# A decoder layer on one core: activations laid out features first by the host, and the first norm's sum by squares and one product with ones

## The chip, the cores and the metric

The kernel runs on one core of one Trainium2 chip. The metric is device time in microseconds of one execution, the median of three runs. A core has five engines that work side by side, each with its own queue of instructions: TensorE (PE; its weight loads are listed as PEld), VectorE (DVE), ScalarE (ACT), GpSimd (POOL) and SyncE (SP), which here only issues transfers. ACT and POOL issue transfers too, on queues of their own.

## The reference, cut to what matters

One decoder layer runs on 256 prompt tokens and on 8 x 8 sample tokens that share the weights, 320 tokens in all, of 2048 features, in float32.

```python
xn = rms_norm(x, g_mix)
z = xn @ w_in            # 8704 columns: B, C, h, q, k, v, gate_c, gate_a
u = c_gate * h_conv
conv_out, conv_state = short_conv(u, conv_prev, w_conv)     # causal, width 3
y_conv = (b_gate * conv_out) @ w_conv_out
attn = ...               # window 128, 16 query and 4 kv heads, bias table, sinks
y_attn = attn @ w_attn_out
merged = sigmoid(gate_c) * y_conv + sigmoid(gate_a) * y_attn
h = x + merged @ w_o
hn = rms_norm(h, g_ffn)
h = h + (silu(hn @ w_gate) * (hn @ w_up)) @ w_down
y = rms_norm(h, g_final)
```

`rms_norm(x, g)` is `x * rsqrt(mean(x * x) + eps) * g`. For the sample group the keys are 128 cached ones of each sequence and 8 new ones, and the convolution starts from two cached rows. Besides y, the updated window of keys and values and the last two rows of u are returned.

## The kernel before

Everything is kept features first: a tile has 128 features as its partitions and the 320 tokens along its rows, and the 2048 features are 16 chunks. A product takes 128x128 of the weights as PE's stationary operand and streams the 320 tokens. Float32 is reached by splitting both sides in a rounded part and a rest (`xh` and `xl`, `whi` and `wlo`) and adding three products: `xh whi`, `xl whi`, `xh wlo`. So each weight tile is loaded by SP (`wraw`, four buffers), its `whi` is made by ACT (L94) and its `wlo` by DVE (L95; three buffers each).

The factor 1/rms is the same for all features of a token. So the products run on x times the gain, and the results are multiplied afterwards by `rb`, a tile that holds 1/rms of each token on all 128 partitions.

x comes in tokens first: three tiles `x0`, `x1`, `x2` of 128, 128 and 64 tokens, in five blocks of columns (`x_load`, L241). For each chunk PE transposes three pieces into PSUM (`x_turn`, L250, tile `pt`), ACT makes `xh` from it (L277; DVE for chunk 0, L275), DVE makes `xl` (L279) and copies x itself to `hT` (L286), which the residual needs later. The gain vector is transposed too (`pv`, L273, L274); `g_ffn` and the convolution's weights follow (`pw`).

The first stage is the product for keys and values (`kv_product`, L327): 16 chunks by 4 column blocks by 3 products, 192 in all, on weight tiles of 1, 1, 2, 2, ... chunks with 512 columns. In the course of a tile the x of the next tile is prepared (`x_prep`). Between products, `tick()` lets a generator of side work take one step. In this stage that is `start_rest`: eight small loads on POOL, which wait behind a copy of one column of `xh` of chunk 3 (`gate`, L344); the squares of x by rows on ACT (L362, twelve of them, each with a sum along the row); the bias table by a small product (`pe_`, L383), whose result `e_sb` goes to memory and back (`e_scr`, L387; `bias_s`, L398); the transposes of the convolution's state (`pst`, L394); and the norm. There 1/rms is worked out on 128x3 values (`rstd_of`, L184 to L196: scale and eps, root on ACT, reciprocal, and a step of refinement), put on the diagonals of three tiles `dg`, and spread over all partitions by three products with ones (`prb`, L409). After the stage `rb` is copied out of PSUM (L417), and the four accumulators are multiplied by it (`kT`, L419; `vT`, L421). Four PSUM banks hold accumulators (`acc`), so `q`, the next product, writes into banks that `kT` has to be read out of first.

Then come `q`, and `C`, `H`, `B` of the convolution, while the side work is attention. `sample_attention` loads the eight sequences' cached keys (`ck`, POOL), transposes them on PE (`pck`, L608, two to a sequence), copies them to `kf` together with the new keys (ACT, L609 and L610) and forms the scores (`pss`, L626). After that come the gates and output products (`gc`, `ga`, `yc`, `ya`), in whose first ticks `conv_state` transposes the last rows of u (`g18`, by `pg`, L837) and sends them out, then `wo`, and the feed-forward network in two halves (`fg`, `fu`, `dn`). The second norm takes its sum of squares by features: POOL squares and adds chunk after chunk (L909, L912, L913, tile `hacc`), one product with ones (`pss`, L992) adds over the partitions, and `rstd_of` runs on 128x320.

The program's order on each engine is laid down when it is built, by priority in the order of the source and by when a planner expects operands to be ready; `after(...)` puts an instruction behind given ones on their engines.

Of the kernel before, what the change touches and what calls it, by code (L numbers as in the profile page):

```python
# [8 lines left out]
F32 = mybir.dt.float32  # L9
# [6 lines left out]
D = 2048  # L16
TP, NB, TS = 256, 8, 8
T = TP + NB * TS
DC = 1024
# [17 lines left out]
LAG = 3  # L37
TOK = [(0, 128), (128, 128), (256, 64)]
# [3 lines left out]
def hybrid_layer(ctx: ExitStack, tc: tile.TileContext, a: dict, o: list):  # L42
    nc = tc.nc
    y_p, y_s, nk_p, nv_p, ncv_p, nk_s, nv_s, ncv_s = o
# [47 lines left out]

    def split_to(hi, lo, src):
        last["hi"] = nc.scalar.activation(hi, src, AF.Copy)  # L94
        last["lo"] = nc.vector.tensor_sub(lo, src, hi.bitcast(F32))  # L95
# [71 lines left out]
    vecs = cst.tile([P, 56], F32, name="vecs")  # L167
    g_mix = vecs[:, 0:16]
    g_ffn = vecs[:, 16:32]
    wcv = vecs[:, 32:56]  # L170
# [31 lines left out]
    hT = xp.tile([P, KC, T], F32, name="hT")  # L202
# [21 lines left out]
    vrow = st.tile([56, P], F32, name="vrow")  # L224
    g_in = nc.gpsimd.dma_start(vrow[0:16, :], a["g_mix"][0].rearrange("(k p) -> k p", p=P))
    with after(g_in):
        nc.gpsimd.memset(ident, 0.0)
    ident_in = nc.gpsimd.affine_select(
# [3 lines left out]
    xs = [st.tile([P, D], F32, name=f"x{t}") for t in range(3)]  # L232
    nc.vector.memset(xs[2][64:, :], 0.0)
    XB = [2, 2, 4, 4, 4]

    def x_load(i):
        cs = slice(sum(XB[:i]) * P, sum(XB[:i + 1]) * P)
        for t, (t0, tn) in enumerate(TOK):
            src = a["x_prompt"][0, t0:t0 + tn, :] if t < 2 else a["x_sample"].flatten_outer_dims()
            eng = nc.scalar if (i, t) in ((0, 1), (0, 2), (1, 2)) else nc.sync  # L240
            eng.dma_start(xs[t][:tn, cs], src[:, cs])  # L241

    x_load(0)
# [4 lines left out]
    def x_turn(kc, pt, tiles=range(3)):  # L248
        for t in tiles:
            last["x"] = nc.tensor.transpose(pt[:, t * P:(t + 1) * P], xs[t][:, kc * P:(kc + 1) * P], ident)  # L250

    def x_first():

        pts = [ps_aux(u("pt")) for _ in range(2)]
        for kc in range(2):
            x_turn(kc, pts[kc], (0, 1))
        with after(last["x"]):
            last["x"] = nc.tensor.matmul(wm, busy[:, :P], busy, start=True, stop=True)
        for kc in range(2):
            with after(last["x"]):  # L260
                x_turn(kc, pts[kc], (2,))
        last.pop("x")
        return pts

    def x_prep(kc, pt=None):
        if pt is None:
            pt = ps_aux(u("pt"))
            with after(last["mm"]):
                x_turn(kc, pt)
            last.pop("x")  # L270
        if kc == 0:
            pv = ps_aux("pv")
            nc.tensor.transpose(pv[:, 0:16], vrow[0:16, :], ident[:16, :16])  # L273
            mark["g"] = nc.vector.tensor_copy(g_mix, pv[:, 0:16])  # L274
            m1 = nc.vector.tensor_scalar(xh_t[:, kc, :], pt[:, :T], g_mix[:, kc:kc + 1], None, op0=ALU.mult)  # L275
        else:
            m1 = nc.scalar.activation(xh_t[:, kc, :], pt[:, :T], AF.Copy, scale=g_mix[:, kc:kc + 1])  # L277
        with after(*(mark[0][1:] if kc == 1 else ())):
            m2 = nc.vector.scalar_tensor_tensor(  # L279
                xl_t[:, kc, :], pt[:, :T], g_mix[:, kc:kc + 1], xh_t[:, kc, :].bitcast(F32),  # L280
                op0=ALU.mult, op1=ALU.subtract,
            )
        mark[kc] = (m1, m2)
        with after(*((last["lo"],) if kc < 2 and "lo" in last else ())):
            for k, p in [(kc, pt)] if kc > 1 else [(0, mark["pt"]), (1, pt)] if kc else ():
                nc.vector.tensor_copy(hT[:, k, :], p[:, :T])  # L286
        mark["pt"] = pt
# [3 lines left out]
    def load_kv(k0, n):  # L291
        raw = wp.tile([P, KT // 2, CK], F32, tag="wraw", name=u("wraw"), bufs=4)
        nc.sync.dma_start(
            raw[:, :n, :], w_in[k0 * P:(k0 + n) * P, O_K:O_K + CK].rearrange("(k p) n -> p k n", p=P)
        )
        hi = wp.tile([P, KT // 2, CK], F32R, tag="whi", name=u("whi"), bufs=3)
        lo = wp.tile([P, KT // 2, CK], F32R, tag="wlo", name=u("wlo"), bufs=3)
        with after(mark[1][0] if k0 == 2 else mark[k0][0], mark[k0][1]):
            split_to(hi[:, :n, :], lo[:, :n, :], raw[:, :n, :])
        return hi, lo  # L300

    def kv_product(tiles, x_after):
# [3 lines left out]
        pts = x_first()  # L306
        x_prep(0, pts[0])
        for i, n in enumerate(tiles):
            hi, lo = load_kv(k0, n)
            if i == 0:  # L310
                x_prep(1, pts[1])
# [5 lines left out]
            for k, c, m in passes(order, k0 + n == KC):  # L317
                kc = k0 + k
                if k0 + n == KC and (k, c, m) == (0, 2, 0):
                    tick()  # L320
# [5 lines left out]
                with after(*((mark["prb"],) if k0 + n == KC and c == 3 else ())):  # L326
                    last["mm"] = nc.tensor.matmul(  # L327
                        ps[c][:, :T], w[:, k, c * P:(c + 1) * P], x(kc),
                        start=(kc == 0 and m == 0), stop=(kc == KC - 1 and m == 2),
                    )  # L330
# [5 lines left out]
    srow = st.tile([2 * NB, DC], F32, name="srow")  # L336
# [5 lines left out]
    def small_loads():  # L342

        behind = nc.gpsimd.tensor_copy(gate, xh_t[:, 3, 0:1].bitcast(F32))  # L344
        with after(behind):
# [4 lines left out]
            nc.gpsimd.dma_start(vrow[16:32, :], a["g_ffn"][0].rearrange("(k p) -> k p", p=P))  # L350
            nc.gpsimd.dma_start(vrow[32:56, :], a["w_conv"][0].rearrange("j (c p) -> (j c) p", p=P))
            nc.gpsimd.dma_start(srow, a["state_conv"][0].rearrange("b j d -> (b j) d"))
            nc.gpsimd.dma_start(blk, a["c_block"])

    ss = st.tile([P, 3, 4], F32, name="ss")
    nc.vector.memset(ss, 0.5)

    def squares(*parts):
        for h, t in parts:
            tn = TOK[t][1]  # L360
            junk = wk.tile([P, 512], F32, tag="junk", name=u("junk"), bufs=1)
            nc.scalar.activation(  # L362
                junk[:tn, :], xs[t][:tn, h * 512:(h + 1) * 512], AF.Square, accum_out=ss[:tn, t, h:h + 1]
            )

    def start_rest():
        yield
        small_loads()
        yield
        with after(mark[3][0]):  # L370
            squares((0, 0), (0, 1))
        yield
        squares((0, 2), (1, 0))
        yield
        squares((1, 1), (1, 2))
        pw = ps_aux("pw")
        nc.tensor.transpose(pw[:, 0:56], vrow, ident[:56, :56])
        nc.vector.tensor_copy(vecs[:, 16:56], pw[:, 16:56])
        yield
        squares((2, 0), (2, 1), (2, 2))  # L380
# [8 lines left out]
        squares((3, 0), (3, 1), (3, 2))  # L389
        s3 = st.tile([P, 3], F32, name="s3")  # L390
        nc.vector.tensor_reduce(s3, ss, axis=AX.X, op=ALU.add)
        pst = ps_aux("pst")
        for c in range(8):
            nc.tensor.transpose(  # L394
                pst[:, c * 16:(c + 1) * 16], srow[:, c * P:(c + 1) * P], ident[:16, :16]
            )
        nc.vector.tensor_copy(st_sb.rearrange("p c s -> p (c s)"), pst[:, 0:128])
# [4 lines left out]
        r3 = rstd_of(s3, [P, 3], "r3", st)  # L402
        yield
        prb = ps_aux("prb")
        mark["rb"] = prb
        for t, (t0, tn) in enumerate(TOK):
            dg = st.tile([P, P], F32, name=f"dg{t}")
            nc.vector.tensor_scalar(dg[:tn, :tn], ident[:tn, :tn], r3[:tn, t:t + 1], None, op0=ALU.mult)
            mark["prb"] = nc.tensor.matmul(  # L409
                prb[:, t0:t0 + tn], ones[:tn, :], dg[:tn, :tn], start=True, stop=True  # L410
            )

    side_work[0] = start_rest()
    ps_kv = kv_product([1, 1] + [2] * 7, {0: (1,), 2: (2,), 3: (3,), 4: (4,)})
    for _ in side_work[0]:
        pass
    nc.vector.tensor_copy(rb, mark["rb"][:, :T])  # L417
# [6 lines left out]
    sp.close()  # L424

# [172 lines left out]
    def sample_attention(sm):  # L598
        def keys(b):
            ck = sm.tile([P, DKV], F32, tag="ckv", name=u("ck"), bufs=8)  # L600
            nc.gpsimd.dma_start(ck, a["cache_k"][0, b].rearrange("t h d -> t (h d)"))
            return ck

        def keys_t(b, ck):
            kf = sm.tile([P, 2, W2], F32, tag="kf", name=u("kf"), bufs=4)
            pk = ps_aux(u("pck"))
            for j in range(2):
                nc.tensor.transpose(pk[:, j * P:(j + 1) * P], ck[:, j * P:(j + 1) * P], ident)  # L608
            nc.scalar.activation(kf[:, :, 0:WIN], pk[:, 0:256].rearrange("p (j k) -> p j k", j=2), AF.Copy)  # L609
# [597 lines left out]
```

## Time and profile before

| | |
|---|---|
| median of 3 runs | 1690.38 us (1690.11 to 1690.67) |
| profiled execution | 1689.65 us, its span 1687.9 us |
| busy in the span | PE 1678.4, DVE 899.3, ACT 655.9, POOL 82.6 us |
| first `kv` product, first `q` product | 7.32 us, 43.13 us |
| moved | 258.16 MB, mean 153 GB/s |

How lines of the profile read: a timeline row is start, duration, engine, line, operation, result and operands, shapes and how many were merged; in brackets stand the idle time of the engine before it and what ended it. A row of groups gives the count, the busy time, the mean in ns, and the engine's idle time ahead of them. In a row of a window stand its length, then busy time and instructions of PE, PEld, DVE, ACT and POOL, the granted clock, the share of the transfer engines, and GB/s. Chain rows give start, length, and what the time went to. An `ACTq` or `SPq` is that engine's queue issuing a transfer.

### The profile page before, as it was taken

The page shows a single profiled execution, that of the slowest core. Times are in us where ns is not written, and L with a number is a line of the kernel's source. Part 1 is how long each engine was busy: PE and PEld are TensorE (multiplying, and loading weights), DVE is VectorE, ACT ScalarE, POOL GpSimd, SP SyncE. Part 2 cuts the span into 40 slices and gives each one's busy share as a digit, 9 for nine tenths or more (in the row PEclk, how much of TensorE's full clock was granted, in tenths as well). Part 3 has the DMA queues.
Part 4 walks back from the last instruction along what each step waited for, and adds up shares of the span by engine and source line. Part 5 has one row for each costly group of instructions (what it writes and reads, how often), then busy time and mean ns, then how long its engine had stood idle before and what let it go on. Part 6 is the DMA issues. An engine that isn't in the chain of part 4 may idle for free.

```text
span 1687.9 us, 26956 instructions
## 1 busy us (share of the span) xinstructions
PE 1678.4 (99%) x11103; PEld 1631.4 (97%) x11103; DVE 899.3 (53%) x1387; ACT 655.9 (39%) x944; POOL 82.6 (5%) x128
## 2 busy tenths in 40 slices
PE   9999999999999999999999999999999999999998
PEld 8999999999999999999999999998888999999887
DVE  7679564444444445556555555554444455555556
ACT  6455443333333333334333333333333333334344
POOL 2001211000000001330000000000000000000000
PEclk9999999999999999999999999999999999999999
DMA  7654545655545554444444444444444444444543
GB/s 228 174 153 135 171 143 157 179 150 150 150 150 150 150 150 150 150 150 150 150 150 150 150 150 150 150 149 151 150 150 150 150 150 150 150 150 150 175 142 109
DMA packets 238371, 258.16 MB, mean 153 GB/s; under 512 B 9210, under 2 KB 212822, under 8 KB 238120
## 3 DMA queue, kind: packets, MB, share of 16 engines
q1 hardware_dynamic: 235784, 250.25, 48.5%
q0 software_dynamic: 2160, 5.93, 1.3%
q8 instruction: 87, 1.43, 0.3%
q14 instruction: 36, 0.29, 0.1%
q10 hardware_dynamic: 304, 0.26, 0.1%
HBM read 253.29 MB, written 5.08 MB: 153 GB/s over the span
## 4 chain that ended last, share of the span: by engine, by line
PE 99%; DVE 0%; ACT 0%; issue 0%; DVEq 0%
PE fu L144 18%; PE fg L144 18%; PE dn L953 9%; PE wo L144 7%; PE gc L144 7%; PE ga L144 7%; PE dn L961 6%; PE C L144 3%; PE B L144 3%; PE H L144 3%; PE q L144 3%; PE yc L144 3%; PE ya L144 3%; PE dl L957 2%; PE kv L327 2%; PE dr L1110 1%
## 5 line engine op out<-in xcount | busy, mean ns | idle before, releaser
L95 DVE TENSOR_TENSOR wlo<-wraw,whi 128x1024 fp32r<-128x1024 f32 (+1 forms) x480 | 569.2, 1188 | 641.0 <-ACT whi L94 632.4
L94 ACT ACTIVATE whi<-wraw 128x1024 fp32r<-128x1024 f32 (+1 forms) x480 | 491.8, 1030 | 808.9 <-PE dn L953 179.0
L953 PE MATMUL dn<-a_t,whi 128*128 128x512 f32 x672 | 230.1, 395 | 0.0
L144 PE MATMUL fu<-hh_t,whi 128*128 128x320 f32 x704 | 212.4, 309 | 0.0
L144 PE MATMUL fg<-hh_t,whi 128*128 128x320 f32 x704 | 212.1, 308 | 0.0
L144 PE MATMUL fg<-hl_t,whi 128*128 128x320 f32 x704 | 212.1, 308 | 0.0
L144 PE MATMUL fu<-hl_t,whi 128*128 128x320 f32 x704 | 212.1, 308 | 0.0
L144 PE MATMUL fg<-hh_t,wlo 128*128 128x320 f32 x704 | 163.7, 308 | 0.0
L144 PE MATMUL fu<-hh_t,wlo 128*128 128x320 f32 x704 | 163.7, 308 | 0.0
L961 PE MATMUL dn<-a_t,wlo 128*128 128x320 f32 x672 | 158.7, 308 | 0.0
L953 PEld LDWEIGHTS dn<-a_t,whi 128*128 128x128 f32 x672 | 125.1, 188 | 24.4 <-issue 0.5
L144 PEld LDWEIGHTS fu<-hh_t,whi 128*128 128x128 f32 x704 | 132.1, 188 | 0.1
L144 PEld LDWEIGHTS fu<-hl_t,whi 128*128 128x128 f32 x704 | 132.0, 188 | 0.1
L144 PEld LDWEIGHTS fg<-hh_t,whi 128*128 128x128 f32 x704 | 132.1, 188 | 0.0
L144 PEld LDWEIGHTS fg<-hl_t,whi 128*128 128x128 f32 x704 | 132.1, 188 | 0.0
L961 PEld LDWEIGHTS dn<-a_t,wlo 128*128 128x128 f32 x672 | 117.9, 188 | 11.6
L144 PEld LDWEIGHTS fg<-hh_t,wlo 128*128 128x128 f32 x704 | 118.6, 188 | 0.0
L144 PEld LDWEIGHTS fu<-hh_t,wlo 128*128 128x128 f32 x704 | 118.6, 188 | 0.0
L144 PE MATMUL gc<-xh_t,whi 128*128 128x320 f32 x256 | 77.4, 310 | 0.0
L144 PE MATMUL ga<-xh_t,whi 128*128 128x320 f32 x256 | 77.4, 310 | 0.0
L144 PE MATMUL ga<-xl_t,whi 128*128 128x320 f32 x256 | 77.4, 310 | 0.0
L144 PE MATMUL gc<-xl_t,whi 128*128 128x320 f32 x256 | 77.3, 310 | 0.0
(305 smaller groups left out, 2773.0 us busy)
## 6 DMA issues: line engine op xcount, KB each, us to landing
wraw<-in_w_in_dram SPq DMA_DIRECT2D x119, 512.0 KB, 3.7
wraw<-in_w_gate_dram SPq DMA_DIRECT2D x88, 512.0 KB, 3.6
wraw<-in_w_up_dram SPq DMA_DIRECT2D x88, 512.0 KB, 3.6
wraw<-in_w_down_dram SPq DMA_DIRECT2D x88, 512.0 KB, 3.7
wraw<-in_w_o_dram SPq DMA_DIRECT2D x32, 512.0 KB, 3.6
wraw<-in_w_in_dram SPq DMA_DIRECT2D x34, 256.0 KB, 3.5
wraw<-in_w_conv_out_dram SPq DMA_DIRECT2D x16, 512.0 KB, 3.5
wraw<-in_w_attn_out_dram SPq DMA_DIRECT2D x32, 256.0 KB, 4.1
```

Of the source, the lines that this page charges most:

```text
L94: last["hi"] = nc.scalar.activation(hi, src, AF.Copy)
L95: last["lo"] = nc.vector.tensor_sub(lo, src, hi.bitcast(F32))
L144: last["mm"] = nc.tensor.matmul(ps[c][:, :T], w[:, k, c * P:(c + 1) * P], x(kc), start=(kc == 0 and i == 0), stop=(kc == nk - 1 and i == 2),)
L327: last["mm"] = nc.tensor.matmul(ps[c][:, :T], w[:, k, c * P:(c + 1) * P], x(kc), start=(kc == 0 and m == 0), stop=(kc == KC - 1 and m == 2),)
L953: nc.tensor.matmul(ps[c], parts[k][0][:, cs], a_t[:, k, 0:512], start=k == 0, stop=False)
L957: nc.tensor.matmul(low[:, :w], a_t[:, k, 512:], parts[k][0], start=k == 0, stop=k == nf - 1)
L961: last["mm"] = nc.tensor.matmul(ps[c][:, :T], parts[k][1][:, cs], a_t[:, k, 0:T], start=False, stop=k == nf - 1)
L1110: last["mm"] = nc.tensor.matmul(ps[:, :CW], x, w, start=(t == 2 and k == 0 and m == 0), stop=(k == nf - 1 and m == len(ms) - 1),)
```

## The change

The host lays out x (both groups), the two gain vectors with the convolution's weights, the convolution's state, and a copy of the cached keys features first, and puts the new convolution state back in order afterwards. On the chip:

- x comes straight into `hT`, now a part of a tile `xv` that begins with 56 columns of vectors, in eight blocks of 1, 1, 2, 2, 2, 2, 2 and 4 chunks, each one transfer of 128 partitions on SP. All transposes of x and of the vectors go, and with them the copies to `hT`. `xh` and `xl` read `hT`.
- The first two weight tiles are loaded on ACT's queue. In the first tile all products of one kind come before those of the next.
- ACT starts with a root of one column.
- The sum of squares: chunk by chunk ACT (even) or DVE (odd) squares 128x320, POOL adds it to `xacc`, and one product with ones adds over the partitions; `rstd_of` then runs on 128x320 and writes `rb` itself. It stands in the tile of chunks 12 and 13.
- The first splits of `q` are put behind the root on ACT and the last step of the norm on DVE (`first`).
- The state's transposes go; its load is direct. Two more small loads go.
- The cached keys are loaded by four transfers straight into `kf`, the new keys are added by two ACT copies, and the key transposes go. The scores keep their ticks.
- `g18` is sent out as it is; its transposes and copies go.

```diff
+VW = 56
+XB = [1, 1, 2, 2, 2, 2, 2, 4]
...
+    first = []
     def split_to(hi, lo, src):
-        last["hi"] = nc.scalar.activation(hi, src, AF.Copy)
-        last["lo"] = nc.vector.tensor_sub(lo, src, hi.bitcast(F32))
+        with after(*first):
+            last["hi"] = nc.scalar.activation(hi, src, AF.Copy)
+            last["lo"] = nc.vector.tensor_sub(lo, src, hi.bitcast(F32))
...
-    hT = xp.tile([P, KC, T], F32, name="hT")
+    xv = xp.tile([P, VW + KC * T], F32, name="xv")
+    g_mix, g_ffn, wcv = xv[:, 0:16], xv[:, 16:32], xv[:, 32:VW]
+    hT = xv[:, VW:].rearrange("p (k t) -> p k t", k=KC)
...
+    def x_load(i):
+        c0, c1 = (VW + sum(XB[:j]) * T if j else 0 for j in (i, i + 1))
+        nc.sync.dma_start(xv[:, c0:c1], a["x_v"][:, c0:c1])
+    x_load(0)
+    x_load(1)
+    first_root = st.tile([P, 1], F32, name="first_root")
+    nc.scalar.activation(first_root, ones[:, 0:1], AF.Sqrt)
...
+    def x_prep(kc):
         if kc == 0:
-            pv = ps_aux("pv")
-            nc.tensor.transpose(pv[:, 0:16], vrow[0:16, :], ident[:16, :16])
-            mark["g"] = nc.vector.tensor_copy(g_mix, pv[:, 0:16])
-            m1 = nc.vector.tensor_scalar(xh_t[:, kc, :], pt[:, :T], ...)
+            m1 = nc.vector.tensor_scalar(xh_t[:, kc, :], hT[:, kc, :], ...)
         else:
-            m1 = nc.scalar.activation(xh_t[:, kc, :], pt[:, :T], AF.Copy, ...)
+            m1 = nc.scalar.activation(xh_t[:, kc, :], hT[:, kc, :], AF.Copy, ...)
...
     def load_kv(k0, n):
-        nc.sync.dma_start(
+        (nc.scalar if k0 < 2 else nc.sync).dma_start(
...
+            seq = passes(order, k0 + n == KC)
+            if i == 0:
+                seq.sort(key=lambda kcm: kcm[2])
+            for k, c, m in seq:
...
-                if k0 and (k, c, m) == (0, 3 if n > 1 else 1, 0) and k0 + n < KC:
+                if k0 and (k, c, m) == (0, 1 if n == 1 or k0 + 2 * n == KC else 3, 0) and k0 + n < KC:
                     x_prep(k0 + n)
                     x_prep(k0 + n + 1)
                     tick()
...
-            nc.scalar.activation(
-                junk[:tn, :], xs[t][:tn, h * 512:(h + 1) * 512], AF.Square, accum_out=...
-            )
+    xacc = st.tile([P, T], F32, name="xacc")
+    def squares(*chunks):
+        for k in chunks:
+            t = xacc if k == 0 else st.tile([P, T], F32, tag="sq", name=u("sq"), bufs=4)
+            if k % 2 == 0:
+                nc.scalar.activation(t, hT[:, k, :], AF.Square)
+            else:
+                nc.vector.tensor_mul(t, hT[:, k, :], hT[:, k, :])
+            if k:
+                nc.gpsimd.tensor_tensor(xacc, xacc, t, op=ALU.add)
...
     def start_rest():
+        squares(0)
         yield
         small_loads()
+        squares(1)
+        yield
+        squares(2, 3, 4)
+        yield
+        squares(5, 6, 7)
+        yield
+        squares(8, 9, 10, 11)
         ...              # nsink, pe_, e_sb, e_scr as before
         yield
+        squares(12, 13, 14, 15)
+        yield
         ...              # bias_s as before
         yield
         prb = ps_aux("prb")
+        nc.tensor.matmul(prb[:, :T], ones, xacc, start=True, stop=True)
+        rstd_of(prb[:, :T], [P, T], "r1", st, out=rb)
...
-    nc.vector.tensor_copy(rb, mark["rb"][:, :T])
...
+    first += [last["root"], last["inv"]]
...
+        kf = sm.tile([P, NB, 2, W2], F32, name="kf")
+        for h in range(0, NB, 2):
+            nc.gpsimd.dma_start(kf[:, h:h + 2, :, 0:WIN], a["cache_kt"][:, h:h + 2])
...
-            ps = product(load_q(j, gp), KC, xh, xl, "q")
+            ps = product(load_q(j, gp), KC, xh, xl, "q", loaded=first.clear)
...
-                nc.tensor.transpose(pg[:18, i * P:(i + 1) * P], g18[:, h * 4 + i, :], ident)
-            nc.vector.tensor_copy(n18[:, h * 512:(h + 1) * 512], pg[:18, :])
...
+        nc.gpsimd.dma_start(ncv, g18)
```

More of the change, by code (lines that the diff above doesn't have):

```diff
@@ L231, in hybrid_layer @@
     )
[L232 to L243, printed above, removed]
     wm = ps_aux("wm")
@@ L247, in hybrid_layer @@
         nc.tensor.matmul(wm, busy[:, :P], busy, start=True, stop=True)
[L248 to L270, printed above, removed]
+    def x_prep(kc):
         if kc == 0:
-            pv = ps_aux("pv")
-            nc.tensor.transpose(pv[:, 0:16], vrow[0:16, :], ident[:16, :16])
-            mark["g"] = nc.vector.tensor_copy(g_mix, pv[:, 0:16])
-            m1 = nc.vector.tensor_scalar(xh_t[:, kc, :], pt[:, :T], g_mix[:, kc:kc + 1], None, op0=ALU.mult)
-        else:
[L277 to L281, printed above, removed]
-            )
+            m1 = nc.vector.tensor_scalar(xh_t[:, kc, :], hT[:, kc, :], g_mix[:, kc:kc + 1], None, op0=ALU.mult)
+        else:
+            m1 = nc.scalar.activation(xh_t[:, kc, :], hT[:, kc, :], AF.Copy, scale=g_mix[:, kc:kc + 1])
+        m2 = nc.vector.scalar_tensor_tensor(
+            xl_t[:, kc, :], hT[:, kc, :], g_mix[:, kc:kc + 1], xh_t[:, kc, :].bitcast(F32),
+            op0=ALU.mult, op1=ALU.subtract,
+        )
         mark[kc] = (m1, m2)
[L284 to L287, printed above, removed]
     CK = 2 * DKV
@@ L325, in kv_product @@
                 w, x = ((hi, xh), (hi, xl), (lo, xh))[m]
[L326 to L330, printed above, removed]
+                last["mm"] = nc.tensor.matmul(
+                    ps[c][:, :T], w[:, k, c * P:(c + 1) * P], x(kc),
+                    start=(kc == 0 and m == 0), stop=(kc == KC - 1 and m == 2),
+                )
             k0 += n
@@ L388, in start_rest @@
         yield
[L389 to L397, printed above, removed]
+        squares(12, 13, 14, 15)
+        yield
         nc.gpsimd.dma_start(
@@ L401, in start_rest @@
         yield
-        r3 = rstd_of(s3, [P, 3], "r3", st)
-        yield
         prb = ps_aux("prb")
[L405 to L411, printed above, removed]
+        nc.tensor.matmul(prb[:, :T], ones, xacc, start=True, stop=True)
+        rstd_of(prb[:, :T], [P, T], "r1", st, out=rb)
     side_work[0] = start_rest()
-    ps_kv = kv_product([1, 1] + [2] * 7, {0: (1,), 2: (2,), 3: (3,), 4: (4,)})
+    ps_kv = kv_product([1, 1] + [2] * 7, {0: (2,), 2: (3,), 3: (4,), 4: (5, 6), 5: (7,)})
     for _ in side_work[0]:
         pass
-    nc.vector.tensor_copy(rb, mark["rb"][:, :T])
     for c in range(2):
@@ L598, in sample_attention @@
     def sample_attention(sm):
[L599 to L609, printed above, removed]
-            nc.scalar.activation(kf[:, :, WIN:W2], kT[:, :, TP + b * TS:TP + (b + 1) * TS], AF.Copy)
-            return kf
+        kf = sm.tile([P, NB, 2, W2], F32, name="kf")
@@ new lines, in sample_attention @@
+        new = kT[:, :, TP:T].rearrange("p j (b t) -> p b j t", b=NB)
+        for j in range(2):
+            nc.scalar.activation(kf[:, :, j, WIN:W2], new[:, :, j], AF.Copy)
+        yield
+        yield
+        for base in range(0, NB, 3):
+            ps = ps_aux(u("pss"))
+            n = min(3, NB - base)
+            for b in range(base, base + n):
+                o0 = (b - base) * W2
+                for kv in range(NKV):
+                    j, par = kv // 2, kv % 2
+                    rows = slice(par * 64, par * 64 + 64)
+                    nc.tensor.matmul(
+                        ps[kv * 32:(kv + 1) * 32, o0:o0 + W2], qs[rows, j, b, :], kf[rows, b, j, :],
+                        start=True, stop=True,
+                    )
+            nc.vector.tensor_add(
+                s[:, base:base + n, :], ps[:, 0:n * W2].rearrange("p (b k) -> p b k", b=n),
+                flip(bias_s).unsqueeze(1).to_broadcast([P, n, W2]),
+            )
@@ L1205 @@
     r = _run(nc, [arrays], core_ids=[0])
-    return tuple(r.results[0][f"out_{i}_dram"] for i in range(len(_OUTS)))
+    res = [r.results[0][f"out_{i}_dram"] for i in range(len(_OUTS))]
+    ncv = _np.asarray(res.pop()).transpose(2, 1, 0)
+    res.insert(4, ncv[:2].reshape(1, 1, 2, DC))
+    return (*res, ncv[2:].reshape(1, NB, 2, DC))
```

89 lines of the change are left out of this document (18 added, 71 removed).

## The prediction

> **What bounds the kernel now.** I read the page first: the span, and the chain that ended last.
>
> ```profile
> span 1687.9 us, 26956 instructions
> ...
> PE 99%; DVE 0%; ACT 0%; issue 0%; DVEq 0%
> ```
>
> TensorE (PE) is the chain from end to end, so whatever leaves its stream leaves the time, unless something else becomes late in its place. The profiled execution took 1689.65 us, 1.75 more than its span; the median of the three runs is 1690.38, 0.73 above it. I work out differences on the trace and take them off 1690.38.
>
> The unit price is in the chain itself, where a whole stretch has no wait in it:
>
> ```profile
> 267.06 14.08 PE H L144 x96
> ```
>
> 96 products of 128x128 weights with 320 tokens in 14.08 us are 0.147 us each. The change is nearly all in the first stage, the product for keys and values (`kv`), so I read its chain from 0 to 46 us, its first and last product in the timeline, and its window:
>
> ```profile
> by line: PE kv L327 64.1%; PE pt L250 12.5%; PE wm L247 6.9%; PE q L144 6.1%; PE prb L409 1.8%; PE pst L394 1.3%; DVE xh_t L275 1.2%; DVE busy L163 1.1%; PE wm L258 0.9%; issue 0.9%; PE pe__406 L383 0.7%; PE pw L377 0.4%; DVE vecs L274 0.4%
> ```
>
> ```profile
> 0.74 0.40 ACTq L241 DMA_DIRECT2D x<-in_x_prompt_dram  x1
> ...
> 1.20 0.44 SPq L293 DMA_DIRECT2D wraw<-in_w_in_dram  x1
> ...
> 4.75 0.63 ACT L94 ACTIVATE whi<-wraw 128x512 fp32r<-128x512 f32 x1 [1.10 <-DMA wraw<-in_w_in_dram]
> ...
> 7.32 0.82 PE L327 MATMUL kv<-xh_t,whi 128*128 128x320 f32 x4 [0.94 <-DVE xh_t L275]
> ...
> 8.87 1.06 ACT L94 ACTIVATE whi<-wraw 128x1024 fp32r<-128x1024 f32 x1 [1.20 <-DMA wraw<-in_w_in_dram]
> ...
> 43.13 0.31 PE L144 MATMUL q<-xh_t,whi 128*128 128x320 f32 x1
> ```
>
> ```profile
> 0.00:7.50 7.50, 5.09 (x16) 2.60 (x17) 3.48 (x7) 2.79 (x4) 1.44 (x9) 1.00 0.76 229
> 0.00:8.85 8.85, 6.44 (x25) 3.96 (x26) 4.83 (x10) 2.96 (x4) 1.44 (x9) 1.00 0.80 251
> 7.32:43.13 35.81, 35.81 (x251) 34.56 (x252) 28.81 (x61) 25.60 (x53) 8.08 (x15) 1.00 0.78 227
> ```
>
> The stage has 192 kv products, 28.2 us at 0.147, but runs 35.81 us, from 7.32 to 43.13. The chain says what fills the rest: `pt`, the transposes of x, 12.5% of 46 us or 5.8; `prb` 0.8, `pst` 0.6, and `pe_` 0.3. VectorE (DVE, third pair of the window row) is busy for 28.81 of the 35.81 us. That is the number to keep in mind: PE is the bound, but DVE is the next one.
>
> **The start.** Three waits stand ahead of the first product at 7.32: the transposes, the gain vector's transpose with its copy, and xh by DVE. With x and gains already feature first, only a load and one DVE pass are left for x, and the first weights decide. Those were issued at 1.20 on SP and used at 4.75, after 3.55 us. They move to ACT's queue, whose first transfer went out at 0.74: there at 4.29, split (0.63) at 4.92, first product at about 5.1, 2.2 us earlier. That is not all kept. The third weight tile (two chunks) could be split at 8.87 before. Ahead of it must come four chunks of x and four of weights, 0.16 and 0.26 MB each, and 0.03 MB of vectors: 1.73 MB, the same as before in another order. The windows say 229 GB/s over the first 7.5 us, 1.72 MB. So it lands between 7.5 and 8.87; I take 8.0, as nothing now has to wait for later chunks of x. Its split (1.06) ends at 9.1. PE, having done 24 products from 5.1, would be there at 8.6; so the third tile starts at 9.1.
>
> **What PE has left.** From 9.1: 14 chunks of 12 products, 168 x 0.147 = 24.7, plus the table product `pe_` and the one product with ones, 0.3 and some 0.8 (the six records of `prb`, also plain f32, took 0.8): the stage could end at 34.9. Against 43.13 that is 8.2 us. Whether it does depends on DVE.
>
> **What DVE gets.** Its groups between 9.1 and 43.1 us:
>
> ```profile
> L95 DVE TENSOR_TENSOR wlo<-wraw,whi 128x1024 fp32r<-128x1024 f32 x7 | 8.5, 1212 | 0.0
> L279 DVE SCALAR_TENSOR_TENSOR xl_t<-pt,vecs,xh_t 128x320 fp32r<-128x320 f32 x14 | 7.6, 545 | 4.7 <-ACT xh_t L277 4.7
> ```
>
> The copies of 16 transposed chunks out of PSUM go. There stay seven `wlo` (8.5) and, after 9.1, twelve `xl` at 0.545 (6.5). New are seven of the eight odd squares and the chain that makes 1/rms, which was on 128x3 values and now runs on 128x320. The same chain on that shape is in the trace, for the second norm:
>
> ```profile
> L192 DVE RECIPROCAL r<-r 128x320 f32<-128x320 f32 x1 | 2.2, 2159 | 0.5 <-ACT r L191 0.5
> ...
> L194 DVE TENSOR_TENSOR r<-r,r 128x320 f32<-128x320 f32 x1 | 0.5, 494 | 0.0
> L196 DVE SCALAR_TENSOR_TENSOR rb<-r,r 128x320 f32<-128x320 f32 x1 | 0.5, 483 | 0.0
> L184 DVE TENSOR_SCALAR r<-pss 128x320 f32<-128x320 f32 x1 | 0.5, 482 | 0.0
> L193 DVE SCALAR_TENSOR_TENSOR r<-r 128x320 f32<-128x320 f32 x1 | 0.5, 479 | 0.0
> ```
>
> That is 2.16 + 0.49 + 0.48 + 0.48 + 0.48 = 4.1. Squares at the price of such a tensor product, 7 x 0.49 = 3.4. For the small steps that stay (the e_sb table, nsink) I allow 0.8. So 8.5 + 6.5 + 3.4 + 0.8 + 4.1 = 23.3 us of DVE's own work.
>
> **What Pool's adds cost DVE.** Fifteen adds of 128x320 on Pool are new here, fourteen after 9.1. The nearest rows are the second norm's sums, first on Pool, then what DVE did at the same time:
>
> ```profile
> 661.03 0.72 POOL L912 TENSOR_TENSOR sq<-hT 128x320 f32<-128x320 f32 x1 [9.45 <-DVE hT L902]
> 661.83 1.04 POOL L913 TENSOR_TENSOR hacc<-hacc,sq 128x320 f32<-128x320 f32 x1
> 662.83 1.75 POOL L912 TENSOR_TENSOR sq<-hT 128x320 f32<-128x320 f32 x1
> ```
>
> ```profile
> 661.58 0.55 DVE L904 SCALAR_TENSOR_TENSOR hl_t<-hT,vecs,hh_t 128x320 fp32r<-128x320 f32 x1 [0.63 <-ACT hh_t L903]
> ...
> 663.92 1.01 DVE L904 SCALAR_TENSOR_TENSOR hl_t<-hT,vecs,hh_t 128x320 fp32r<-128x320 f32 x1
> ```
>
> The two engines hold each other up. A Pool operation takes 0.72 when it meets little of DVE and 1.75 beside a `wlo`; the DVE operation takes 1.01 instead of 0.55 after meeting Pool, 0.46 more. The bounds for an add are therefore nothing (it falls in an idle gap of DVE) and 0.72 (DVE stands for all of it); I take the measured 0.46: 14 x 0.46 = 6.4.
>
> [...]
>
> **The sum.** DVE is through its list at 9.1 + 23.3 + 6.4 = 38.8, and the first key bank must then be scaled before `q` may write into it, 0.5: `q` starts at 39.3 instead of 43.13, 3.8 us earlier. PE's own 34.9 is covered by it. ACT loses its twelve row squares and gets eight of 128x320, and stays behind both. The wait put on the first splits of `q` (behind the root on ACT and the last step of the norm on DVE) costs nothing by itself as those two come before the scaling that `q` needs anyway; what is queued behind them is the first `q` tile. Pool's adds stand in one queue with six loads and the e_scr transfer:
>
> ```profile
> 10.99 0.19 POOL L344 COPY gate<-xh_t 128x1 f32<-128x1 f32 x1 [8.47 <-ACT xh_t L277]
> ...
> 14.74 0.56 POOL L353 DMA_DIRECT2D blk<-in_c_block_dram  x1
> 28.99 0.52 POOL L387 DMA_DIRECT2D e_scr<-e_sb  x1 [13.68 <-DVE e_sb L386]
> ```
>
> The gate can open some 2 us earlier, six loads at about 0.55 end near 12.3, and fourteen adds at 1.04, the middle row, with 0.5 for e_scr, end at 27.4: before the product with ones is due.
>
> Later parts, both on the chain between dense products, so that removing them is all gain (chains of 200 to 228 us, and from 296):
>
> ```profile
> by line: PE C L144 50.3%; PE H L144 27.4%; PE pss L626 8.1%; PE B L144 7.3%; PE pck L608 7.3%
> ```
>
> ```profile
> 298.74 0.87 PE pg L837 x8
> ```
>
> The key transposes are 7.3% of 28 us, 2.0; the conv state's are 0.9. What replaces them is four loads on Pool instead of eight and two ACT copies instead of sixteen; the scores stay at the same ticks.
>
> Together 3.8 + 2.0 + 0.9 = 6.7 us: 1683.7.
>
> **Rivals.** *PE stays the bound.* DVE idled for 7.0 us of the old stage (35.81 - 28.81); if the adds fall into such gaps and the chain on 128x320 runs beside the last tile, the stage ends at 34.9 and the gain is 8.2 + 2.9 = 11.1: 1679.3. Against it: DVE's list alone is 23.3 of 25.8 us. 0.27.
>
> [...] Each add costs DVE 0.72: 10.1 instead of 6.4, `q` at 43.0, the stage gains nothing and only the later parts remain: 1687.4. [...] 0.20 with what lies between.
>
> *Pool's queue stops PE (slower).* e_scr waited until 28.99 for e_sb. If eight adds queue behind it, from 29.5 at 1.75 (the row beside a `wlo`) they end at 43.5. The product with ones stands in PE's queue ahead of the last 45 kv products, so PE stands still: 43.5 + 0.6 + 6.6 = 50.7, 7.6 later than before, less 2.9: 1695.1. It decides for slower when the last add ends after 42.2. For it: one queue, one chain of sums. Against it: half the adds come ahead of e_scr, and e_sb can come earlier as its loads do. 0.05.
>
> **How the numbers follow.** The forecast has 0.45, with `q` between 37 and 41.5. The range runs from the first rival, 1679, to past the second, 1688; it leaves out the third and 0.03 for what I don't see. This kernel's runs differ by some 0.03%; 0.2%, or 3.4 us, is about what can be told from no change. Faster by more means below 1687.0: the forecast, the first rival and half of the second, 0.82. Within it the other half and the unseen, 0.13. Slower 0.05.
>
> **What would show it.** Right: first kv product near 5.1, third tile near 9.1, no `pt`, `pck`, `pg` on PE; DVE over 90% busy from there until `q`; `wlo` and `xl` lengthened beside Pool's adds; PE gaps of some 4 us in the stage, ended by `wlo` or `xl`; `q` near 39.3. Wrong: PE gaps ended by Pool's last add (third rival), or no gaps at all (first).

## The result and the profile after

The changed kernel takes 1690.89 us, the median of 14 runs (1689.51 to 1691.37), against 1690.43 (1689.14 to 1691.18) for the kernel before in 14 runs: a ratio of 1.0001, 95% interval 0.9994 to 1.0009. The forecast was 1683.7, with a range from 1679.0 to 1688.0. Nothing was gained that can be measured, and the measured time lies outside the range.

The profiled execution took 1691.36 us. Its page, the span and the chain that ended last:

```profile
span 1689.3 us, 26708 instructions
...
PE 98%; DVE 1%; DMA 0%; POOL 0%; issue 0%; SPq 0%; ACT 0%; DVEq 0%; POOLq 0%
```

The span is 1.4 us longer than before, and the chain, which was PE with hardly anything else, now has a percent of DVE and traces of Pool. They lie in the first stage. Its timeline on PE, with the first products, the first product after each of the two long gaps, and the window of the stage:

```profile
5.15 1.44 PE L296 MATMUL kv<-xh_t,whi 128*128 128x320 f32 x4 [0.52 <-ACT whi L99]
...
9.58 0.47 PE L296 MATMUL kv<-xh_t,whi 128*128 128x320 f32 x1
9.85 0.47 PE L296 MATMUL kv<-xl_t,whi 128*128 128x320 f32 x1
...
11.24 0.31 PE L296 MATMUL kv<-xh_t,whi 128*128 128x320 f32 x1
11.38 0.31 PE L296 MATMUL kv<-xl_t,whi 128*128 128x320 f32 x1
...
23.34 0.31 PE L296 MATMUL kv<-xl_t,whi 128*128 128x320 f32 x1
25.24 0.42 PE L296 MATMUL kv<-xh_t,wlo 128*128 128x320 f32 x1 [1.59 <-DVE wlo L100]
...
28.74 0.31 PE L296 MATMUL kv<-xl_t,whi 128*128 128x320 f32 x1
33.81 0.64 PE L296 MATMUL kv<-xh_t,wlo 128*128 128x320 f32 x1 [4.77 <-DVE wlo L100]
```

```profile
5.15:10.64 5.49, 5.49 (x20) 5.49 (x21) 4.66 (x8) 4.81 (x10) 2.96 (x6) 1.00 1.00 374
5.15:45.70 40.55, 34.19 (x196) 33.10 (x197) 36.20 (x46) 20.38 (x37) 24.19 (x28) 0.92 0.65 212
31.12:37.95 6.83, 4.14 (x15) 4.14 (x16) 6.50 (x6) 0.00 (x0) 3.32 (x4) 0.50 0.63 168
```

The first product came at 5.15 as forecast, 2.17 earlier than before. But `q` starts at 45.70, 2.57 later than before: the stage lasts 40.55 us instead of 35.81. Four things fill it beside its 28.2 us of products at full pitch. The first twenty products take 5.49 us, 0.27 each (9.58 to 9.85) where later ones take 0.147, 2.5 more than at that pitch; the clock's records begin at 10.64, at full speed, and ahead of the first one the column shows 1.00 for these products too, so there the pitch has to tell: it is that of the products from 34.24 to 37.18, in the stretch granted half. PE stands for 1.90 and for 5.07 us start to start, both times until a `wlo` comes from DVE; 6.7 less the two products themselves. From 31.12 to 37.95 the clock is granted at half, and the 18 products behind the second gap take 4.76 us (the chain, below), 2.1 too many. `prb` and `pe_` make 0.8. That is 28.2 + 2.5 + 6.7 + 2.1 + 0.8 = 40.3 of the 40.55.

What DVE did ahead of the second gap is in the chain of waits:

```profile
23.57 1.61 DVE wlo L100
25.18 2.16 DVE xl_t L253 x2
27.34 0.80 DVE sq L330
...
29.75 1.14 DVE xl_t L253
30.89 1.07 DVE sq L330
31.96 1.81 DVE wlo L100
...
33.81 4.76 PE kv L296 x18
38.58 0.54 PE prb L360 x2
```

The `wlo` that PE needs stands in DVE's queue behind four `xl` and two squares of later chunks, and each of these takes about twice what it takes without Pool beside it (`xl` 0.55 us, a square 0.48, in the run without adds below). The groups of the first 46 us on DVE and Pool:

```profile
L253 DVE SCALAR_TENSOR_TENSOR xl_t<-xv,xh_t 128x320 fp32r<-128x320 f32 x16 | 12.8, 832 | 0.0
L100 DVE TENSOR_TENSOR wlo<-wraw,whi 128x1024 fp32r<-128x1024 f32 x7 | 10.8, 1558 | 0.5 <-ACT whi L99 0.5
L330 DVE TENSOR_TENSOR sq<-xv 128x320 f32<-128x320 f32 x8 | 5.8, 738 | 1.3 <-POOL xacc L332 1.3
```

```profile
L332 POOL TENSOR_TENSOR xacc<-xacc,sq 128x320 f32<-128x320 f32 x15 | 16.8, 1120 | 1.3 <-DVE sq L330 0.5
```

`xl` takes 832 ns where it took 545 before, `wlo` 1558 for 1212, and an add on Pool 1120. ACT, which was to stay behind, waits as well; its waits from 9 to 30 us:

```profile
ACT sq L328 <- POOL xacc L332: 5.6, 3, 2.1
```

Three squares on ACT stand for 5.6 us until an add on Pool lets go of one of the four `sq` buffers, and in ACT's order the next `xh` and `whi` stand behind them.

### The profile page after: what moved, and what is told of

It is laid out like the page before. It is cut to its first block, busy times and chain, and to the rows that moved or that the text cites. A ratio compares the mean times of both kernels' runs of the same rounds, so it can differ in the third digit from the quotient of the medians.

```text
span 1689.3 us, 26708 instructions
## 1 busy us (share of the span) xinstructions
PE 1673.3 (99%) x11016; PEld 1626.4 (96%) x11016; DVE 903.9 (54%) x1367; ACT 647.4 (38%) x914; POOL 95.8 (6%) x135
## 4 chain that ended last, share of the span: by engine, by line
PE 98%; DVE 1%; DMA 0%; POOL 0%; issue 0%; SPq 0%; ACT 0%; DVEq 0%; POOLq 0%
PE fg L149 18%; PE fu L149 18%; PE dn L883 9%; PE ga L149 7%; PE wo L149 7%; PE gc L149 7%; PE dn L891 6%; PE H L149 3%; PE C L149 3%; PE B L149 3%; PE q L149 3%; PE ya L149 3%; PE yc L149 3%; PE dl L887 2%; PE dr L1040 1%; PE kv L296 1%
## 5 line engine op out<-in xcount | busy, mean ns | idle before, releaser
L149 PE MATMUL wo<-m_h,whi 128*128 128x320 f32 x256 | 77.2, 309 | 0.0
```

Source lines behind the costliest of these rows:

```text
L149: last["mm"] = nc.tensor.matmul(ps[c][:, :T], w[:, k, c * P:(c + 1) * P], x(kc), start=(kc == 0 and i == 0), stop=(kc == nk - 1 and i == 2),)
```

## The experiments

Two theories stand against each other. **A**: the loss comes from Pool's adds, through the time that they and DVE take from each other and through the `sq` buffers that they hold. **B**: it comes from the squares themselves, work added to DVE and ACT ahead of what PE needs. The expectations name a third one, **C**: the slow clock of the first products makes the loss. Ratios are against the kernel before, with 95% intervals.

**Without the adds, and without squares and adds.**

```diff
             # e1_no_adds
-            if k:
-                nc.gpsimd.tensor_tensor(xacc, xacc, t, op=ALU.add)
             # e2_no_squares
+            if k:
+                continue
```

> Leaves out Pool's fifteen adds, so the norm's sum holds chunk 0 alone; the squares, the product with ones and the rest stay. Theory A (Pool's adds starve DVE: each holds up a DVE operation for about half a microsecond, and an unread square holds up ACT and DVE): xl falls back to 0.55 us and wlo to 1.2, the two PE gaps (1.9 and 5.1 us) go, the clock is not taken back, q starts at 36 to 38 instead of 45.7, and the time is about 1682. Rival B (DVE's own longer list, with squares ahead of wlo in its queue, is what PE waits for): the gaps stay at over half their length, q at 42 or later, time over 1686.5. Rival C (the clock at half rate from 5.1 to 10.6 makes the loss): q about 2 us earlier than 45.7 at most.

> Leaves out the squares of chunks 1 to 15 and their adds; the product with ones and the 1/rms chain on 128x320 stay. Theory A: hardly better than without the adds alone, at most 1 us (1681 to 1682), since DVE then has idle time already. Rival B: here the gap goes, and this kernel is 4 us or more faster than the one without adds.

Measured: 1680.57 us without the adds, 0.9941 (0.9926 to 0.9956); 1680.42 without squares and adds, 0.9943 (0.9928 to 0.9958). The groups of the first 46 us of the kernel without adds:

```profile
L100 DVE TENSOR_TENSOR wlo<-wraw,whi 128x1024 fp32r<-128x1024 f32 x7 | 8.5, 1224 | 1.9 <-ACT whi L99 1.9
L253 DVE SCALAR_TENSOR_TENSOR xl_t<-xv,xh_t 128x320 fp32r<-128x320 f32 x16 | 8.2, 549 | 0.0
L330 DVE TENSOR_TENSOR sq<-xv 128x320 f32<-128x320 f32 x8 | 3.8, 480 | 0.0
```

All the lengthening is gone with the adds, and so is every gap on PE; `q` starts at 35.17, 10.5 earlier than with them, near the difference of the times (10.3). Taking the squares away too brings nothing more. B falls.

Not all of the 10.5 belongs to the adds, as the two executions start differently: without the adds the full clock came at 5.75 instead of 10.64 (the first four products took 0.97 us instead of 1.23, the next four 0.58 instead of 1.07). The profiled execution without squares and adds had the slow start too (0.27 us from product to product up to 10.54, `q` at 36.96); it took 1682.29 us where its three other runs took 1680.26 to 1680.55. Against that one the change, also with a slow start, is 9.1 us longer.

**More buffers for the squares.** The wait of ACT and DVE for a free buffer is taken away by giving every square its own.

```diff
-tag="sq", name=u("sq"), bufs=4)
+tag="sq", name=u("sq"), bufs=15)
```

> Fifteen buffers for the squares instead of four, so no square waits for an add. If the queue behind the four buffers is the larger part of theory A, ACT's waits on Pool (1.7, 2.1, 1.7 us) go, the PE gaps shrink to under 2 us together, q at 40 or earlier, time about 1685. [...]

Measured: 1696.51 us, 1.0037 (1.0023 to 1.0051), 5.6 slower than the change and `q` at 49.95. No theory had expected that. DVE's timeline, and the chain of waits of the same stretch:

```profile
24.32 1.00 DVE L253 SCALAR_TENSOR_TENSOR xl_t<-xv,xh_t 128x320 fp32r<-128x320 f32 x2
25.24 0.47 DVE L330 TENSOR_TENSOR sq<-xv 128x320 f32<-128x320 f32 x1
25.64 1.00 DVE L253 SCALAR_TENSOR_TENSOR xl_t<-xv,xh_t 128x320 fp32r<-128x320 f32 x2
...
30.17 1.20 DVE L100 TENSOR_TENSOR wlo<-wraw,whi 128x1024 fp32r<-128x1024 f32 x1
42.41 0.49 DVE L185 TENSOR_SCALAR r<-prb 128x320 f32<-128x320 f32 x1 [11.04 <-PE prb L360]
```

```profile
22.37 9.73 POOL xacc L332
...
40.02 0.88 POOL xacc L332
40.90 0.04 issue
40.95 1.43 PE prb L360 x2
```

From 22.6 to 31.4 DVE works back to back, and at its undisturbed lengths (two `xl` in 1.00, a `wlo` in 1.20), while one single add on Pool takes 9.73 us. It ends at 32.10, 0.73 after DVE's last instruction. The adds behind it, with DVE idle, take 0.86 to 0.88 each, so by these numbers it did nearly all of its work only then; that is an estimate, as no view shows how far an add has got. With four buffers the longest of the fifteen adds took 1.73 us. Everything behind it on Pool is late, the last add ends at 40.9, and PE stands from 30.83 to 40.95 at the product with ones. With four buffers DVE and ACT had to wait for Pool (1.3 and 5.6 us), and the author's reading is that these waits had let Pool in; the number of buffers is all that differs between the two kernels, but no run shows the waits' part by itself.

**The adds on DVE.**

```diff
-                nc.gpsimd.tensor_tensor(xacc, xacc, t, op=ALU.add)
+                nc.vector.tensor_tensor(xacc, xacc, t, op=ALU.add)
```

> The fifteen adds run on DVE instead of Pool, behind each square; nothing is left out. If it is the meeting of the two engines that costs (theory A), 15 x 0.49 = 7.3 us more of DVE work is cheaper than Pool's adds: no xl over 0.6 us, PE gaps shorter than 7.0 us together, q at 40 to 42, time about 1686 to 1688. If it were the mere amount of work ahead of wlo (rival B), the gaps would stay and q come at 45 or later, time 1690 or more.

Measured: 1683.19 us, 0.9957 (0.9942 to 0.9972); `q` at 38.96. The group of the adds:

```profile
L332 DVE TENSOR_TENSOR xacc<-xacc,sq 128x320 f32<-128x320 f32 x15 | 7.2, 479 | 0.0
```

DVE does the same sums in 0.48 each, and with `xl` back at 544 ns the kernel is 7.7 us faster than with the adds on Pool. In the profiled execution, the slowest of the four (1684.49), one gap of 2.3 us is left, at 21.58.

**Pool busy, but reading nothing.** In place of each add Pool fills the square's buffer with zeros: the same queue, the same buffers, the same order.

```diff
-                nc.gpsimd.tensor_tensor(xacc, xacc, t, op=ALU.add)
+                nc.gpsimd.memset(t, 0.0)
```

> Leaves out the adds; in the place of each, Pool overwrites the square's tile with zeros, so Pool's queue keeps as many instructions, each waiting for its square and freeing its buffer, but none that reads. If DVE and Pool exclude each other through what they read, DVE's xl and wlo go back to 0.55 and 1.2 us, q at about 36, time 1681 to 1682 as without the adds. If the order and the waits of Pool's queue, or any Pool access, cost the time, PE gaps of 3 us or more stay and the time is over 1685.

Measured: 1680.77 us, 0.9942 (0.9927 to 0.9957); `q` at 35.02. Its groups of the first 46 us, on DVE and Pool:

```profile
L253 DVE SCALAR_TENSOR_TENSOR xl_t<-xv,xh_t 128x320 fp32r<-128x320 f32 x16 | 8.1, 541 | 0.0
```

```profile
L332 POOL MEMSET sq<- 128x320 f32 x15 | 5.1, 376 | 1.4 <-DVE sq L330 1.3
```

Fifteen zero fills on Pool between the same instructions leave DVE's operations at their lengths: `xl` at 541 ns and `wlo` at 1211, where fifteen adds went with 832 and 1558; a square takes 512, against 480 without adds and 738 with them. So in this run neither the queue nor the order lengthens DVE's operations, nor does a write of 128x320 by Pool; what the add has beyond the fill is that it reads two tiles in SBUF and computes, and no run parts those two. A zero fill is also shorter, 0.38 us against 0.86 or more for an add, and gives the buffers back sooner (ACT's 5.6 us of waits are gone); so this run doesn't tell how much of the loss came through the lengthening and how much through the held buffers. Who is held up is not the same in all runs either: with four buffers both were (`xl` 832 ns, an add 1120), with fifteen DVE kept its lengths from 22.6 to 31.4 and the add took 9.73 us.

**A longer warm-up.** Two more `wm` products ahead of the stage, against the twenty slow products at the start.

```diff
-    for _ in range(7):
+    for _ in range(9):
```

> Nine warming products instead of seven, so that PE is busy until the first kv product at about 5.3 us. If the clock is granted by how busy PE was before, it is full at about 6 instead of 10.6 and 20 products take 0.147 instead of 0.267 us. Theory A: the gain is waited away at the later gaps, which grow by as much; q within 0.7 us of 45.7, time the same as 1690.9. Rival C: q 2 us or more earlier, time about 1688.5.

Measured: 1690.01 us (10 runs), 0.9995 (0.9986 to 1.0004), 0.9 less than the change, and the two intervals overlap. In the profiled execution, which took 1688.99, the products ran at full pitch from the first one on, at 5.34 (0.69 us for the first four, 0.59 for the next), and `q` came at 43.15, 2.5 earlier than A had put it; the two gaps were 2.7 and 2.9 us. So the slow start is a loss of its own in an execution that has it, some 2 us (`q` at 36.96 and 35.17 in the first two experiments say the same), which A had denied. But it comes and goes, and most of C's loss is not there: the median gained less than half of the 1.9 us that this execution did.

**The sum on PE.** ACT squares all chunks, rounded, and sixteen products with ones add them up in `prb`; nothing is left for DVE or Pool. The same again with nine warm products.

```diff
...
-            if k % 2 == 0:
-                nc.scalar.activation(t, hT[:, k, :], AF.Square)
-            else:
-                nc.vector.tensor_mul(t, hT[:, k, :], hT[:, k, :])
-            if k:
-                nc.gpsimd.tensor_tensor(xacc, xacc, t, op=ALU.add)
+            nc.scalar.activation(t, hT[:, k, :], AF.Square)
+            nc.tensor.matmul(prb[:, :T], ones_r, t, start=k == 0, stop=k == KC - 1)
...
```

> All sixteen squares on ACT, written in the rounded format, and added up over chunks and partitions by sixteen products with ones into one PSUM bank; no squares on DVE, no adds on Pool. PE pays 16 x 0.147 = 2.3 us for the 0.5 of the product that goes. Theory A: no PE gap over 0.6 us, q at 36.5 to 38.5, time 1682 to 1684, some 7 us under the kernel before.

> The same with nine warming products instead of seven. If the clock's grant at the start varies from execution to execution with seven (5.8, 6.9, 10.5, 10.6 us in four profiles), and comes by 6 with nine, then as DVE no longer holds PE up the 2.4 us of a late grant show in the time: up to 2 us faster than with seven in those executions, 0 in the others, and a narrower spread.

Measured: 1683.50 us, 0.9958 (0.9943 to 0.9972), `q` at 38.16, and with nine warm products 1682.23, 0.9950 (0.9934 to 0.9967), `q` at 36.62; the full pitch came at 9.17 and with the first product, at 4.96 (0.69 us for the first four, 0.59 for the next). The stage runs without a gap of more than 0.2 us; sixteen products of 0.147 (2.4 us) stand on PE for the one with ones.

**The place of the tiles.** All kernels so far, the change included, lose 1.4 us late, in the feed-forward's second product and behind it. The groups of `dn` before, after, and in the second run below:

```profile
L953 PE MATMUL dn<-a_t,whi 128*128 128x512 f32 x672 | 230.1, 395 | 0.0
L961 PE MATMUL dn<-a_t,wlo 128*128 128x320 f32 x672 | 158.7, 308 | 0.0
```

```profile
L883 PE MATMUL dn<-a_t,whi 128*128 128x512 f32 x672 | 231.0, 396 | 0.0
L891 PE MATMUL dn<-a_t,wlo 128*128 128x320 f32 x672 | 159.5, 309 | 0.0
```

```profile
L879 PE MATMUL dn<-a_t,whi 128*128 128x512 f32 x672 | 230.1, 395 | 0.0
L887 PE MATMUL dn<-a_t,wlo 128*128 128x320 f32 x672 | 158.8, 308 | 0.0
```

The code of these products is unchanged; their tiles lie elsewhere in SBUF, since the tiles ahead of them changed size. Two runs on the kernel above with the warm-up shift them: one makes the vectors' part of `xv` 64 columns wide and adds a strip of 56 columns ahead, the other widens `xv` alone.

```diff
-VW = 56
+VW = 64
...
+    room = cst.tile([P, 56], F32, name="room")     # in the first of the two only
```

> The kernel with the sum on PE and nine warming products, plus two unused strips that put the weight tiles and the a_t tiles where they stood before, modulo 64 bytes (56 columns in the first pool, the vectors' 56 columns made 64). In the profiles so far the dn and dr products of all changed kernels took 1.4 us longer than before (672 products at 234.0 and 672 at 147.2 ns against 233.2 and 146.2). If the place of the tiles does it, dn and dr go back to before's length and the time is about 1680.8. If something else does, they keep it and the time is 1682.2.

> The same without the strip in the first pool: weight tiles stay where the changed kernel has them, and the tiles behind x move by 32 bytes. If it is the weight tiles' place that lengthens dn, it stays 1 us longer than before, time about 1682; if it is the place of the tiles behind x, dn changes.

Measured: 1681.62 us, 0.9947 (0.9932 to 0.9962), and 1681.58, 0.9947 (0.9930 to 0.9963). In both `dn` has its old length again (third fence). What is left of the 1.4 us is the end: from DVE's last operation to the end of the span it is 4.7 us in all of these kernels, against 4.2 before, in which the results are sent out; why is open. The time fell by 0.6 and not by the 1.0 of `dn`, as `q` came 0.7 and 0.9 later in these two executions. What the two share is that the tiles behind x lie 32 bytes further on. Which tile it is, and by what rule, stays open.

**Squares on ACT, pairs on DVE, eight products on PE.** From what the runs show, on the first of the two placements:

```diff
...
-            if k:
-                nc.gpsimd.tensor_tensor(xacc, xacc, t, op=ALU.add)
+            nc.scalar.activation(t, hT[:, k, :], AF.Square)
+            if k % 2:
+                s2 = st.tile([P, T], F32R, tag="sq2", name=u("sq2"), bufs=4)
+                nc.vector.tensor_add(s2, mark["sq"], t)
+                nc.tensor.matmul(prb[:, :T], ones_r, s2, start=k == 1, stop=k == KC - 1)
+            mark["sq"] = t
...
```

> On top of both strips: DVE adds the squares in pairs (8 x 0.49 = 3.9 us), and PE sums eight tiles instead of sixteen, 8 x 0.147 = 1.2 us less. If DVE has the room that the theory gives it without Pool (20 us of its own in the 26 us from the third tile on), no wlo comes late and q starts 1.2 us earlier, time about 1 us under the kernel with both strips. If DVE is full again, PE gaps of over 0.5 us appear and the gain is lost.

Measured: 1680.95 us (1680.76 to 1680.99), 0.9943 (0.9928 to 0.9958), 9.5 less than the kernel before in the same runs. The window of its stage:

```profile
5.31:36.36 31.05, 31.05 (x203) 30.25 (x203) 29.23 (x50) 23.06 (x45) 6.91 (x13) 1.00 0.89 288
```

PE is busy for all of the stage's 31.05 us, without a wait. DVE has nearly as much work as in the forecast's sum, 29.2 us, and it costs nothing, as none of it is lengthened or late.

## Why the prediction was wrong, point by point

**The start** held: 5.1 forecast, 5.15 measured. **The third tile at 9.1** did not: its 24 predecessors were not done at 8.6 but at about 11.2, at 0.27 us each instead of 0.147. The clock was left out of the working. Before, the records show full speed from 5.94, ahead of the first product at 7.32; with the first product at 5.15 the stage itself ran at the slow pitch, until 10.64 in this execution. That is not the same in every execution: with the same start, the run without adds had the full clock at 5.75.

**DVE's own list**, 23.3 us, was right: without the adds its operations take the forecast lengths (549, 1224 and 480 ns).

**Pool's adds** are the step that failed, in size and in kind. In size: against the run without adds, `xl` grew by 283 ns sixteen times, `wlo` by 334 seven times and the squares by 258 eight times, 8.9 us or 0.59 for each of the fifteen adds; 0.46 was taken, fourteen times, 6.4. That is 2.5 us too little, and the smaller part. The upper bound of 0.72 was low as well: that row is a multiplication that reads one tile, and an add by itself takes 0.86 to 0.88 (fifteen buffers, from 32.18 on). In kind: the working added the adds up into one list that DVE goes through without a stop, with PE idle for the 4.4 us between 34.9 and 39.3. But the order counts. The lengthened `xl` and squares of chunks to come stand ahead of the `wlo` that PE needs at once, so PE stood for 6.7 us, and behind the second gap it got half the clock, 2.1 more. That delayed the product with ones to 38.58, so DVE, through with its list at 37.6 and 26.98 us busy of the 28.5 before, then waited 1.53 for PE and had the norm's 4.1 still ahead. PE and DVE took turns where the sum had them side by side. In the end PE came last and not DVE: its 46 products from 39.12 on ran without a stop up to `q` at 45.70, and beside them DVE had `rb` at 43.9 and the first key bank scaled by 44.9. No run changed the order in DVE's queue alone, so what the order cost is read from the trace and not measured by itself. Stops, half clock and slow start together cost 11.3 us, where the sum had 4.4.

**ACT "stays behind both"** failed: the four `sq` buffers, which the working did not look at, held it for 5.6 us.

**Pool's queue**: the adds were to end at 27.4 and ended at 34.5:

```profile
28.03 0.54 POOL L351 DMA_DIRECT2D e_scr<-e_sb  x1
...
33.38 1.10 POOL L332 TENSOR_TENSOR xacc<-xacc,sq 128x320 f32<-128x320 f32 x1
```

`e_scr` itself stood behind eleven adds, and four more came behind it. At 38.58 the product with ones had its operand, so the third rival did not decide here. With fifteen buffers PE did stand at that product until Pool's last add, and the time was 1696.5; that this is near the rival's 1695.1 is luck, as one add of 9.73 us did it and not eight adds behind `e_scr`.

**The later parts** held: the two stretches with the keys' transposes, from their first product to the next stretch's, went from 17.61 to 17.02 us and from 17.14 to 16.04 (2.0 forecast, 1.7 measured), the conv state's from 14.95 to 14.08 (0.9 and 0.87). The 1.4 us that `dn` and the end took back were not foreseen.

**The sum**: 2.2 at the start gained, 4.7 in the stage lost, 2.6 later gained, 1.4 lost in `dn` and at the end: 1.4 longer in the traces, as the spans say. **The rivals**: the first, that PE stays the bound, 1679.3 with `q` at 34.9, is what the kernel does without the adds: 1680.57 and 35.17. The second, 0.72 us of DVE for each add, came nearest in time (1687.4), but it too had only added up lengths; no run shows 0.72, and 0.59 for each add were measured. Only the third had PE stop, at the product with ones; none had the stops for a `wlo`, and none the clock.

## What to carry to other kernels

An engine with time to spare is not free if its work slows the engine next to the bound: fifteen adds of 320 columns on Pool cost this kernel some 9 us in executions with like starts, on DVE itself 2.6, and about 1 as pairs on DVE with eight products on PE (a stage of 31.05 us, against 30.06 with no adds at all). A sum of durations per engine is not enough where queues run in order: look at what stands ahead of the instruction that the bound waits for, and price each stop of PE with the clock that it can lose (2.1 us behind the gap of 5.07 here). More buffers are no cure by themselves: here fifteen instead of four made the kernel 5.6 us slower, with one add of 9.73 us.

## What the runs showed of the hardware

Stops of PE can cost more than their length: behind the gap of 5.07 us after the change 18 products took 2.1 us more than at full pitch. The granted clock in three more windows, behind a gap of 2.7 us (nine warm products), of 2.3 us (adds on DVE) and of 10.1 us (fifteen buffers):

```profile
25.54:28.95 3.41, 3.41 (x15) 3.41 (x14) 3.41 (x4) 3.30 (x6) 3.17 (x4) 0.50 0.53 154
```

```profile
24.93:28.35 3.42, 3.42 (x15) 3.42 (x14) 3.42 (x8) 1.06 (x1) 1.70 (x3) 0.50 0.94 231
```

```profile
34.20:44.44 10.24, 3.50 (x11) 3.10 (x12) 1.49 (x2) 1.50 (x3) 6.55 (x9) 0.50 0.35 92
```

With the 6.83 us after the change, these are one, two and three times 3.41. Counted from the start of the last product ahead of the gap, the half clock came 2.4 us later after the change and 3.4 with fifteen buffers, both still in the gap; with nine warm products and with the adds on DVE it came behind the gap's end, by 0.34 and 1.05 us. The gap of 1.90 after the change cost no clock: its window, from 23.34 to 25.24, is granted 1.00, and so is the time from there to 31.12. Nor did the second gap with nine warm products cost any, from 30.21 to 33.12, though at 2.91 us it was the longer of the two there:

```profile
30.00:45.00 15.00, 12.40 (x82) 11.78 (x80) 14.36 (x21) 3.83 (x7) 5.11 (x6) 1.00 0.62 148
```

So the length of a gap alone does not tell whether the clock is halved; what does was not shown. Nor was it shown why the full clock comes at different times with seven warm products: at 5.75 without the adds, at 9.17 by the pitch with the sum on PE, at 10.64 after the change. That may also be what spreads the runs of before and after over 2 us each; it was not tested.

A `dn` product took about 1 ns longer after the change (means of 396 and 309 ns against 395 and 308) and had its old length again with the tiles behind x 32 bytes further on; 1344 of them made 1.0 of the 1.4 us lost late: enough to count in a comparison at this level.
